# Strassen's seven products for both projections, dealt to the engines by a planner

## Chip, core and metric

The kernel runs on one core of one Trainium2 chip. The metric is the device time of one execution in microseconds (us), lower is better. Engines are named as the profile names them: PE multiplies matrices, DVE (VectorE), ACT (ScalarE) and POOL (GpSimd) do elementwise work, SP only issues transfers (DMA).

## What is computed

One layer of a decoder trunk in float32: `x` is 1024 x 2048, `w_in` 2048 x 6144, `w_out` 2048 x 2048.

```python
h = einsum('bsd,de->bse', x, w_in)                 # 1024 x 2048 x 6144
q, k, v, u_pool, gate = split(h, [1024, 2048, 3072, 4096])
attn = dilated_attention_mixture(rotary(q), rotary(k), v)   # 8 heads of 128
pool_out = grouped(causal_mean(u_pool, (2, 4, 8, 16)) - u_pool, w_pool) * pool_scale
y = concatenate([attn, pool_out]) * silu(gate)
out = einsum('bse,ed->bsd', y, w_out)              # 1024 x 2048 x 2048
x = layer_norm(2 ** 0.25 * x + out) * ln_gain + ln_bias
```

## The kernel before

**Products.** PE reads numbers in a shortened 32-bit type (fp32r), so each float32 tile is split in two: `hi`, a copy by ACT (L108, `ACT.activation(hi, src, AF.Copy)`), and `lo`, the rest, by DVE (L109, `DVE.tensor_tensor(out=lo, in0=src, in1=hi, op=ALU.subtract)`, two inputs in on-chip memory, SBUF). A product of two tiles is then three matmuls, `hi*hi + hi*lo + lo*hi`, added up in a bank of PSUM (512 columns each, 8 banks).

**Input projection.** `x` is loaded and split once at the start and stays in SBUF (`h`, `l`). The weights come in pieces of 128 x 512 (`Pieces`), loaded by SP (L127) and split up to four pieces ahead of their use. One block of 128 output columns after another runs over all 16 slices `kc` of 128 rows: q, k, u and gate blocks with the weights stationary and 512 columns of `x` moving (L640), value blocks with `x` stationary and 256 columns moving (L633). A block leaves PSUM once, when its 16 slices are done.

```python
for n, (a, b) in enumerate(((wh, xh), (wh, xl), (wl, xh))):
    for f in range(2):
        c = slice(f * 512, f * 512 + 512)
        PE.matmul(t[f], a[:, es], b[kc][:, c], start=kc == 0 and n == 0,
                  stop=kc == KC - 1 and n == 2)
```

**The second stream.** Attention of a head (L317 to L403: scores, softmax, transposes, products with the values) and pooling (L437 to L516) are cut into steps that `Background` lays between the units of the projection: `bg.tick()` after each slice. The order is thus fixed in the source. POOL does 32 multiplications for the rotary turn (L265, 32 x 512), a few fills, the roots of the norm (L681) and four pieces of the last norm (L710, L713).

**Output projection and norm.** `y` goes through DRAM (`y_d`), is split, and `mm3` (L731) multiplies it with pieces of `w_out`, four blocks of 128 tokens per piece. `residual` (L670, L671) adds `x` and takes the statistics; `norm` (L684, L688) centres and scales 512 columns at a time on DVE. The last 128 tokens are done in two halves of 256 columns, so that what is left behind the last matmul is one row block: `whole()` shares it between DVE, POOL and ACT.

Of the kernel before, what the change touches and what calls it, by code (L numbers as in the profile page):

```python
# [32 lines left out]
class Background:  # L33
    """Steps of a second stream, laid between the units of the first."""

    def __init__(self, rate):
        self.steps = deque()
        self.rate = rate
        self.credit = 0.0
        self.held = []  # L40

    def later(self, fn, ticks):
        self.held.append([ticks, fn])

    def flush(self):
        for _, fn in self.held:
            fn()
        self.held = []

    def add(self, fn, tag=None):  # L50
        self.steps.append((fn, tag))

    def tick(self):
        for h in self.held:
            h[0] -= 1
        while self.held and self.held[0][0] <= 0:
            self.held.pop(0)[1]()
        if not self.steps:
            self.credit = 0.0
            return  # L60
        self.credit += self.rate
        while self.credit >= 1.0 and self.steps:
            self.credit -= 1.0
            self.steps.popleft()[0]()

    def drain(self, tag=None):
        if tag is not None and all(t != tag for _, t in self.steps):
            return
        while self.steps:
            fn, t = self.steps.popleft()  # L70
            fn()
            if tag is not None and t == tag:
                return
# [3 lines left out]
def kernel(  # L77
    ctx: ExitStack,
    tc: tile.TileContext,
    x_t: bass.AP,  # L80
# [23 lines left out]
    v_d = [dram.tile([6 * P, 2 * P], F32, name=f"v_d{c}") for c in range(2)]
    gp_d = [dram.tile([P, S], F32, name=f"gp_d{c}") for c in range(4)]

    def split(hi, lo, src):
        ACT.activation(hi, src, AF.Copy)  # L108
        DVE.tensor_tensor(out=lo, in0=src, in1=hi, op=ALU.subtract)  # L109

    class Pieces:
        """Weights in pieces of 512 columns: loaded, then split, ahead of their use."""

        def __init__(self, sources, n_raw, n_split):
            self.sources = sources
            self.n_raw = n_raw
            self.n_split = n_split
            self.raw = deque()
            self.ready = deque()
            self.loaded = 0  # L120
            self.made = 0
            self.done = 0

        def load(self):
            if self.loaded < len(self.sources):
                t = wp.tile([P, 512], F32, name="w_raw", bufs=self.n_raw)
                SP.dma_start(t, self.sources[self.loaded])  # L127
                self.raw.append(t)
                self.loaded += 1

        def split(self):
            if self.made < len(self.sources):
                t = self.raw.popleft()
                hi = wp.tile([P, 512], F32R, name="w_hi", bufs=self.n_split)
                lo = wp.tile([P, 512], F32R, name="w_lo", bufs=self.n_split)
                split(hi, lo, t)
                self.ready.append((hi, lo))
                self.made += 1
                self.load()

        def load_first(self, between):
            t = wp.tile([P, 512], F32, name="w_raw", bufs=self.n_raw)
            SP.dma_start(t[:, 0:P], self.sources[0][:, 0:P])
            between()
            SP.dma_start(t[:, P:], self.sources[0][:, P:])
            self.raw.append(t)
            self.loaded = 1

        def split_first(self, between):
            t = self.raw.popleft()  # L150
            hi = wp.tile([P, 512], F32R, name="w_hi", bufs=self.n_split)
            lo = wp.tile([P, 512], F32R, name="w_lo", bufs=self.n_split)
            split(hi[:, 0:P], lo[:, 0:P], t[:, 0:P])
            between()
            split(hi[:, P:], lo[:, P:], t[:, P:])
            self.ready.append((hi, lo))
            self.made = 1
            self.load()

        def fill(self):  # L160
            while self.made < len(self.sources) and self.made - self.done < self.n_split:
                self.split()

        def take(self):
            while not self.ready:
                self.split()
            return self.ready.popleft()

        def retire(self):
            self.done += 1  # L170
# [701 lines left out]
```

## Time and profile before

| | us |
|---|---|
| three timed runs | 1565.46, 1565.57, 1566.03 |
| median of them | 1565.57 |
| span of the profiled execution, first to last instruction | 1564.2 |
| PE busy in it | 1551.0 (99%) |
| DVE, ACT, POOL busy | 631.6, 446.2, 54.6 |

The span is the whole of what the profile has of its execution; the median lies 1.4 us above it, for what is around the first and last instruction. Busy time of PE is the union of its matmuls, each of which is shown longer than the distance to the next one, because they are pipelined.

### The profile page before, as it was taken

The numbers are of one execution on the slowest core, as the hardware profiler recorded it, in microseconds if no ns is written. First come the engines' busy times: TensorE is split into PE (matmuls) and PEld (weight loads), VectorE is DVE, ScalarE is ACT, GpSimd is POOL, SyncE is SP. The second block draws the span as 40 slices with busy tenths as digits, with TensorE's granted clock in tenths as the row PEclk, the third lists the DMA queues.
The fourth block names the chain that finished last, engine by engine and source line by source line (L and its number), as shares of the span: only waits on it lengthen the run. The fifth ranks groups of instructions, "written<-read, shape, count | busy, mean of one in ns | idle before, by whom it ended". The sixth has DMA issues, their size and how long they took to land.

```text
span 1564.2 us, 20097 instructions
## 1 busy us (share of the span) xinstructions
PE 1551.0 (99%) x8116; PEld 1308.5 (84%) x8116; DVE 631.6 (40%) x1155; ACT 446.2 (29%) x788; POOL 54.6 (3%) x59
## 2 busy tenths in 40 slices
PE   9999999999999999999999999999999999999997
PEld 7898889888899888998888888888888888888886
DVE  4362433233441434424342113454153435476446
ACT  4333232142431323323323113222132424222310
POOL 0010100001000000000000000000000000000001
PEclk9999999999999999999999999999999999999999
DMA  7431213311124111241111222222213557357512
GB/s 239 146 110 34 61 41 89 107 35 41 54 68 128 41 41 54 60 117 57 38 54 54 68 75 84 97 75 61 61 54 114 167 205 242 115 197 242 146 52 104
DMA packets 73085, 149.75 MB, mean 96 GB/s; under 512 B 8288, under 2 KB 12256, under 8 KB 71712
## 3 DMA queue, kind: packets, MB, share of 16 engines
q1 hardware_dynamic: 72704, 148.19, 30.6%
q8 instruction: 63, 1.03, 0.3%
q10 hardware_dynamic: 288, 0.29, 0.1%
q14 instruction: 30, 0.25, 0.1%
HBM read 126.42 MB, written 22.02 MB: 95 GB/s over the span
## 4 chain that ended last, share of the span: by engine, by line
PE 98%; DVE 1%; ACT 1%; issue 0%; DMA 0%; DVEq 0%; SPq 0%
PE mm_ps L640 54%; PE mm_ps L731 10%; PE mm_ps L633 10%; PE s_ps L731 6%; PE o_ps L731 3%; PE t_ps L731 3%; PE s_ps L633 1%; PE s_ps L502 1%; PE s_ps L320 1%; PE o_ps L381 1%; PE o_ps L396 1%; PE s_ps L327 1%; PE o_ps L640 1%; PE o_ps L397 1%; PE t_ps L640 1%; PE t_ps L368 0%
## 5 line engine op out<-in xcount | busy, mean ns | idle before, releaser
L109 DVE TENSOR_TENSOR w_lo<-w_raw,w_hi 128x512 fp32r<-128x512 f32 (+1 forms) x337 | 234.3, 696 | 643.8 <-ACT w_hi L108 643.7
L108 ACT ACTIVATE w_hi<-w_raw 128x512 fp32r<-128x512 f32 (+1 forms) x337 | 212.0, 630 | 806.0 <-PE mm_ps L640 426.3
L640 PE MATMUL mm_ps<-h,w_hi 128*128 128x512 f32 x1248 | 395.9, 398 | 0.0
L640 PE MATMUL mm_ps<-l,w_hi 128*128 128x512 f32 x1248 | 386.1, 391 | 0.0
L640 PE MATMUL mm_ps<-h,w_lo 128*128 128x512 f32 x1248 | 386.0, 390 | 0.0
L640 PEld LDWEIGHTS mm_ps<-h,w_lo 128*128 128x128 f32 x1248 | 234.6, 188 | 50.3
L640 PEld LDWEIGHTS mm_ps<-l,w_hi 128*128 128x128 f32 x1248 | 234.5, 188 | 50.0
L640 PEld LDWEIGHTS mm_ps<-h,w_hi 128*128 128x128 f32 x1248 | 225.6, 188 | 45.7 <-issue 4.0
L633 PE MATMUL mm_ps<-w_hi,h 128*128 128x256 f32 x448 | 128.3, 286 | 0.0
L633 PE MATMUL mm_ps<-w_hi,l 128*128 128x256 f32 x448 | 126.8, 283 | 0.0
L633 PE MATMUL mm_ps<-w_lo,h 128*128 128x256 f32 x448 | 126.7, 283 | 0.0
L633 PEld LDWEIGHTS mm_ps<-w_hi,h 128*128 128x128 f32 x448 | 85.9, 192 | 0.5
L633 PEld LDWEIGHTS mm_ps<-w_lo,h 128*128 128x128 f32 x448 | 85.9, 192 | 0.1
L633 PEld LDWEIGHTS mm_ps<-w_hi,l 128*128 128x128 f32 x448 | 85.8, 192 | 0.0
L731 PE MATMUL mm_ps<-w_hi,h 128*128 128x512 f32 x192 | 74.7, 389 | 0.0
L731 PE MATMUL mm_ps<-w_lo,h 128*128 128x512 f32 x192 | 74.7, 389 | 0.0
L731 PE MATMUL mm_ps<-w_hi,l 128*128 128x512 f32 x192 | 74.7, 389 | 0.0
L731 PE MATMUL s_ps<-w_hi,h 128*128 128x512 f32 x128 | 49.8, 389 | 0.0
L731 PE MATMUL s_ps<-w_lo,h 128*128 128x512 f32 x128 | 49.8, 389 | 0.0
L731 PE MATMUL s_ps<-w_hi,l 128*128 128x512 f32 x128 | 49.8, 389 | 0.0
L342 ACT ACTIVATE p_t<-p_t,nm 128x128 f32<-128x128 f32 (+3 forms) x64 | 35.9, 562 | 32.1 <-DVE nm L335 31.7
L333 DVE CUSTOM_DVE_ANT_0 p_t<-s_ps,mask 128x128 f32<-128x128 f32 (+3 forms) x64 | 31.4, 490 | 28.1 <-PE s_ps L327 25.7
(176 smaller groups left out, 1704.7 us busy)
## 6 DMA issues: line engine op xcount, KB each, us to landing
w_raw<-in_w_in_dram SPq DMA_DIRECT2D x159, 256.0 KB, 2.7
w_raw<-in_w_out_dram SPq DMA_DIRECT2D x112, 256.0 KB, 2.7
w_raw<-in_w_v_dram SPq DMA_DIRECT2D x64, 256.0 KB, 2.7
z<-in_x_n_dram SPq DMA_DIRECT2D x8, 1024.0 KB, 5.1
p_t<-in_x_t_dram SPq DMA_DIRECT2D x15, 512.0 KB, 5.4
out_dram<-z SPq DMA_DIRECT2D x30, 256.0 KB, 3.4
y_d<-p_t SPq DMA_DIRECT2D x8, 512.0 KB, 3.8
y_d<-v_f SPq DMA_DIRECT2D x8, 512.0 KB, 3.5
```

The lines of the kernel that those rows point to most:

```text
L108: ACT.activation(hi, src, AF.Copy)
L109: DVE.tensor_tensor(out=lo, in0=src, in1=hi, op=ALU.subtract)
L320: PE.matmul(s[e][:, n - 2 * P:n], a[:, b * P:b * P + P], k[:, b * P - P:b * P + P], start=j == 0, stop=j == 2)
L327: PE.matmul(s[e][NF * r:NF * r + NF, :width(b) - 2 * P], qf[:, q0:q0 + NF], kv[:, :b - 1, r, :], start=True, stop=True, tile_position=(0, ...
L333: DVE.tensor_tensor_reduce(out=pt, in0=s[e][:, :n], in1=mask[:, NM - n:], op0=ALU.add, op1=ALU.max, scale=1.0, scalar=-3.0e38, accum_out=mx)
L342: ACT.activation(pt, pt, AF.Exp, scale=SCALE, bias=st.pop(("m", m, e)), accum_out=den)
L381: PE.matmul(o[:, 0:2 * P], v[:, 2 * m], p[:, 1:3], start=True, stop=False)
L396: PE.matmul(ov[:, e], v[:, 0, r], far_t[0][:, :, c], start=True, stop=False)
L397: PE.matmul(ov[:, e, 4:6], v[0:64, 1, r], far_t[1][:, :, c], start=False, stop=True)
L633: PE.matmul(o, x[kc][:, ss], y[:, es], start=kc == 0 and n == 0 and b % 2 == 0, stop=kc == KC - 1 and n == 2 and b % 2 == 1)
L640: PE.matmul(t[f], a[:, es], b[kc][:, c], start=kc == 0 and n == 0, stop=kc == KC - 1 and n == 2)
L731: PE.matmul(o, a[:, k % 2, ss], b, start=k == 0 and n == 0, stop=k == KC - 1 and n == 2)
```

## The change

**Seven products.** Each big product is cut in 2 x 2 quarters and done by Strassen's scheme (in the form with few sums): seven products of quarters and sums of quarters in place of eight. A *unit* is one of the seven for one piece of output: 4 slices x 3 matmuls of 512 columns in one bank (`mul_pair` for q, k, u, gates; `mul_wide` with `x`, and `y` in the output projection, stationary). There are 448 units: 20 pairs of blocks x 7 x 2 halves of the inner dimension, values 4 x 7 x 2, output 16 x 7. That is 5376 matmuls of 512 columns.

**What it adds.** Sums of quarters of `x`, `w_in`, `w_v`, `w_out` and `y` are made on the chip, nearly all on POOL (`combine`, L369; `w_out`'s and half of `x`'s are made early and laid in DRAM; `y`'s at L691). Every sum or quarter is split as before (L356, L359). Every unit's result leaves PSUM and is added into one or more quarters of the output: the first by an ACT copy (L404) and POOL sums, the others by DVE adds with one input in PSUM (L398). All 20 pairs are done for the first half of the inner dimension (phase A), laid in DRAM (`q_d`) and read again for the second half (phase B). The output projection comes in phases C and D, for attention and pooling. The scores are one float32 matmul instead of three fp32r ones (L762). The rotary turn moves from POOL to transfers and DVE (L717 to L723). The norm of the last four row blocks falls together at the end.

**The planner.** `Plan.op` records every operation with its engine, a due key and a cost in us; `place` gives the tiles their slots; `arrange` deals the operations to engines by a list schedule over those costs, and the program is written in that order. An engine runs its own list in order. Three banks serve a pair's seven units: product 2 is added onto product 1 in its bank, so it has to wait for the ACT copy of product 1; 7 and 4 go onto 6; 3 goes onto 5.

```diff
-class Background:
-    """Steps of a second stream, laid between the units of the first."""
...
+    LATE = {"PE": 1.2, "DVE": 0.3, "ACT": 0.3, "POOL": 0.3, "SP": 0.3}
+
+    def arrange(self):
...
+                    pick = r[0][2]
...
+                    o.start, o.end = t, t + cost
+                    free[e] = o.end
...
+        return sorted(out, key=lambda o: (o.start, o.seq))
...
+PAIRS = [("u", 0), ("g", 0), ("u", 1), ("p", 0), ("u", 2), ("u", 3), ("qk", 0), ("g", 1), ("qk", 1), ("qk", 2),
+         ("g", 2), ("qk", 3), ("qk", 4), ("g", 3), ("qk", 5), ("qk", 6), ("qk", 7), ("p", 1), ("p", 2), ("p", 3)]
...
+    def split(key, t, name, prio=None, lo=0, n=512, into=None):
...
+        def left():
+            DVE.tensor_tensor(out=c.lo(), in0=t.f(lo, lo + n), in1=c.hi(), op=ALU.subtract)
...
+    def combine(eng, key, a, b, alu, name, prio=None, into=None):
+        t = sb(name) if into is None else into
+
+        def go():
+            ENG[eng].tensor_tensor(out=t.f(), in0=a.f(), in1=b.f(), op=alu)
...
+        def take(self, i):
+            name = "abc"[{1: 0, 2: 0, 6: 1, 7: 1, 4: 1, 5: 2, 3: 2}[i]]
+            new = i in (1, 6, 5)
+            if new:
+                self.bank[name] = bank("mm")
+            return self.bank[name], new
...
+            if i == 1:
+                self.x = sb("x1")
+                self.copy(u, self.x, 0, 0, t)
+                if self.loaded:
+                    for q in (1, 3, 2):
+                        self.add("POOL", u, q, self.x)
+                return
+            if self.loaded:
+                self.add("DVE", u, {2: 0, 6: 1, 3: 1, 5: 3, 7: 3, 4: 2}[i], t)
...
+            s[1] = combine("POOL", k1, raw[2], raw[3], ADD, "w_sum")
+            s[2] = combine("POOL", k2, s[1], raw[0], SUB, "w_sum")
+            s[3] = combine("POOL", k3, raw[0], raw[2], SUB, "", into=raw[2])
...
+                    s[4] = combine("POOL", k4, raw[1], s[2], SUB, "", into=raw[1])
...
+                for n, (a, b) in enumerate(((w.hi(), x.hi()), (w.hi(), x.lo()), (w.lo(), x.hi()))):
+                    PE.matmul(o.f(), a[:, es], b, start=new and kc == 0 and n == 0, stop=kc == 3 and n == 2,
+                              skip_group_check=True)
...
+            seq += [(n, 1)] + ([(n - 1, 4)] if n > n0 else []) + [(n, i) for i in (6, 5, 2, 7, 3)]
...
+            if last and d != 3 or not last and d % 2:
...
+                op("DVE", u + 1.4 + 0.3 * d, V5, centred, [mv, gain[d // 2]], [t])
+                op("DVE", u + 1.6 + 0.3 * d, V5, scaled, [rs, bias[d // 2]], [t])
+            else:
...
+                op("ACT", u + 1.8, A5, normal, [nb, rs], [t])
+                op("POOL", u + 2, G5, gained, [gain[d // 2]], [t])
+                op("POOL", u + 2.2, G5, biased, [bias[d // 2]], [t])
```

Three places in the lists of engines. First POOL at the start of the program, before the change (`far_t` is a fill, the rest the rotary turn of head 0):

```order
L240 MEMSET far_t_98 128x768
L241 MEMSET far_t_99 64x256
L265 ISA
L265 TENSOR_TENSOR k_f<-k_f,rope 32x512 x2
L265 TENSOR_TENSOR q_f<-q_f,rope 32x512 x4
```

The same place on POOL in the changed kernel (`x_sum` and `w_sum` are sums of quarters; sums that write `w_raw` overwrite a quarter that is no longer needed):

```order
L369 TENSOR_TENSOR x_sum<-x_raw 128x512 x3
L369 TENSOR_TENSOR w_sum<-w_raw 128x512
L369 TENSOR_TENSOR w_sum<-w_sum,w_raw 128x512
L369 TENSOR_TENSOR x_sum<-x_raw 128x512
L369 TENSOR_TENSOR w_sum<-w_raw 128x512
L369 TENSOR_TENSOR w_sum<-w_sum,w_raw 128x512
L369 TENSOR_TENSOR w_sum<-w_raw 128x512
L369 TENSOR_TENSOR w_sum<-w_sum,w_raw 128x512
L369 TENSOR_TENSOR w_raw<-w_raw 128x512 x3
L369 TENSOR_TENSOR w_raw<-w_raw,w_sum 128x512 x3
```

POOL, which had two fills before its first real work, now has sums to make that the fifth and later products of the first pairs are split from.

Second, DVE in phase A of the changed kernel, about one pair's worth (`q` is a quarter of output, `x_1547` the copy of product 1, `mm` a bank):

```order
L398 TENSOR_TENSOR q<-x_1547,mm 128x512
L359 TENSOR_TENSOR w<-w_raw,w 128x512
L398 TENSOR_TENSOR q<-x_1547,mm 128x512
L359 TENSOR_TENSOR w<-w_sum,w 128x512 x2
L359 TENSOR_TENSOR w<-w_raw,w 128x512
L398 TENSOR_TENSOR q<-q,mm 128x512
L359 TENSOR_TENSOR w<-w_raw,w 128x512 x2
L398 TENSOR_TENSOR q<-q,mm 128x512
L359 TENSOR_TENSOR w<-w_raw,w 128x512
L398 TENSOR_TENSOR q<-x_1547,mm 128x512
```

Before, DVE's list in the projection is splits (`w_lo`, `w_raw` and `w_hi` in SBUF) and a head's steps between them:

```order
L399 TENSOR_TENSOR p_t<-o_ps,p_t 128x2x6x32
L403 TENSOR_TENSOR p_t<-p_t,gate 128x1024
L109 TENSOR_TENSOR w_lo<-w_raw,w_hi 128x512 x12
L260 STREAM_SHUFFLE k_f<-mm_ps 32x512 x2
L264 TENSOR_TENSOR mm_ps<-mm_ps,rope 32x512 x2
L109 TENSOR_TENSOR w_lo<-w_raw,w_hi 128x512
L269 TENSOR_TENSOR mm_ps<-mm_ps,k_f 32x512 x2
L274 TENSOR_TENSOR k_lo<-mm_ps,k_hi 128x512
```

An add that frees a bank, which came once for 16 slices, now stands between any two splits.

Third, DVE behind the last matmul. Before, from the add of the last half row block on:

```order
L670 SCALAR_TENSOR_TENSOR z<-z,s_ps 128x256
L671 BN_STATS stats<-z 128x6
L679 BN_AGGR mv<-stats 128x2
L680 TENSOR_SCALAR rs<-mv 128x1
L704 TENSOR_SCALAR neg<-mv 128x1
L684 SCALAR_TENSOR_TENSOR z<-z,mv,gain 128x512 x2
L688 SCALAR_TENSOR_TENSOR z<-z,rs,bias 128x512
L684 SCALAR_TENSOR_TENSOR z<-z,mv,gain 128x464
L688 SCALAR_TENSOR_TENSOR z<-z,rs,bias 128x512
L688 SCALAR_TENSOR_TENSOR z<-z,rs,bias 128x464
```

And in the changed kernel, from the add of the last unit on, up to the statistics of the last row block (after these rows, 10 more of L1069 and L1073 follow):

```order
L398 TENSOR_TENSOR z<-z,mm 128x512
L1069 SCALAR_TENSOR_TENSOR z<-z,mv,gain 128x512
L1061 SCALAR_TENSOR_TENSOR nb<-mv,rs 128x1
L1069 SCALAR_TENSOR_TENSOR z<-z,mv,gain 128x512
L1073 SCALAR_TENSOR_TENSOR z<-z,rs,bias 128x512 x2
L1069 SCALAR_TENSOR_TENSOR z<-z,mv,gain 128x512
L1073 SCALAR_TENSOR_TENSOR z<-z,rs,bias 128x512
L1069 SCALAR_TENSOR_TENSOR z<-z,mv,gain 128x512 x2
L1073 SCALAR_TENSOR_TENSOR z<-z,rs,bias 128x512 x2
L1043 BN_STATS stats<-z 128x6
L1054 BN_AGGR mv<-stats 128x2
L1055 TENSOR_SCALAR rs<-mv 128x1
```

The norm of two row blocks stands ahead of the statistics of the last two, so four row blocks are finished where one was; POOL's list has 12 sums of 128x512 for the same four.

## Rows read from the trace of the kernel before

**Rows 1.** The page: span, busy time of each engine; the chain that ended last.

```profile
span 1564.2 us, 20097 instructions
...
PE 1551.0 (99%) x8116; PEld 1308.5 (84%) x8116; DVE 631.6 (40%) x1155; ACT 446.2 (29%) x788; POOL 54.6 (3%) x59
...
PE 98%; DVE 1%; ACT 1%; issue 0%; DMA 0%; DVEq 0%; SPq 0%
```

**Rows 2.** The chain in order of time: start, length (us), matmuls with 512 and 256 columns.

```profile
by line: PE mm_ps L640 54.1%; PE mm_ps L731 10.4%; PE mm_ps L633 10.4%; PE s_ps L731 6.3%; PE t_ps L731 2.8%; PE o_ps L731 2.8%; PE s_ps L633 1.5%; PE s_ps L502 1.4%; PE s_ps L320 1.3%; PE o_ps L381 0.9%; PE o_ps L396 0.9%; PE s_ps L327 0.8
...
74.77 23.04 PE mm_ps L633 x192
...
1248.02 43.52 PE mm_ps L731 x192
```

**Rows 3.** Timeline of PE's first products: start, length, engine, line.

```profile
4.60 0.76 PE L640 MATMUL t_ps<-h,w_hi 128*128 128x512 f32 x1
...
6.78 0.63 PE L640 MATMUL o_ps<-l,w_hi 128*128 128x512 f32 x1
7.21 0.63 PE L640 MATMUL t_ps<-h,w_lo 128*128 128x512 f32 x1
```

**Rows 4.** Groups by line and shape: count, busy us, mean ns, idle time before.

```profile
L109 DVE TENSOR_TENSOR w_lo<-w_raw,w_hi 128x512 fp32r<-128x512 f32 x335 | 233.5, 698 | 640.7 <-ACT w_hi L108 640.7
...
L108 ACT ACTIVATE w_hi<-w_raw 128x512 fp32r<-128x512 f32 x335 | 211.1, 631 | 805.3 <-PE mm_ps L640 426.3 <-PE o_ps L731 86.7 <-PE mm_ps L633 83.5
...
L265 POOL TENSOR_TENSOR k_f<-k_f,rope 32x512 f32<-32x512 f32 x16 | 20.2, 1281 | 386.9 <-DVE k_f L260 386.9
...
L274 DVE TENSOR_TENSOR k_lo<-mm_ps,k_hi 128x512 fp32r<-128x512 f32 x16 | 10.7, 686 | 9.2 <-ACT k_f L271 9.2
```

**Rows 5.** Timeline of DVE, 90.6 to 94.5 us.

```profile
91.32 1.24 DVE L109 TENSOR_TENSOR w_lo<-w_raw,w_hi 128x512 fp32r<-128x512 f32 x1
92.48 0.68 DVE L264 TENSOR_TENSOR t_ps<-t_ps,rope 32x512 f32<-32x512 f32 x1
```

**Rows 6.** Timeline of POOL in the same stretch.

```profile
90.72 2.98 POOL L265 TENSOR_TENSOR q_f<-q_f,rope 32x512 f32<-32x512 f32 x2 [8.23 <-DVE q_f L260]
```

**Rows 7.** Timeline of DVE in the end, 1540 to 1565 us.

```profile
1543.63 0.74 DVE L684 SCALAR_TENSOR_TENSOR z<-z,mv,gain 128x512 f32<-128x512 f32 x1
...
1553.32 0.42 DVE L670 SCALAR_TENSOR_TENSOR z<-z,s_ps 128x256 f32<-128x256 f32 x1 [2.62 <-PE s_ps L731]
...
1556.02 1.28 DVE L688 SCALAR_TENSOR_TENSOR z<-z,rs,bias 128x512 f32<-128x512 f32 x1
1557.22 1.19 DVE L684 SCALAR_TENSOR_TENSOR z<-z,mv,gain 128x464 f32<-128x464 f32 x1
1558.33 2.38 DVE L688 SCALAR_TENSOR_TENSOR z<-z,rs,bias 128x512 f32<-128x512 f32 x2
```

**Rows 8.** Timeline of POOL in the end; PE's last matmul.

```profile
1555.82 2.10 POOL L710 TENSOR_TENSOR z<-z,gain 128x288 f32<-128x288 f32 x2
1557.88 2.35 POOL L713 TENSOR_TENSOR z<-z,bias 128x288 f32<-128x288 f32 x2
...
1553.01 0.28 PE L731 MATMUL s_ps<-h,l 128*128 128x256 f32 x1
```

**Rows 9.** Transfers: the queue's share (page), a load's time to land, SP's issue (ns).

```profile
q1 hardware_dynamic: 72704, 148.19, 30.6%
...
w_raw<-in_w_in_dram SPq DMA_DIRECT2D x159, 256.0 KB, 2.7
...
L127 SPq DMA_DIRECT2D w_raw<-in_w_in_dram x159: 327/328/548, 2.6 to 1161.7; - x159
```

**Rows 10.** Windows: busy us (count) of each engine, PE's clock, transfers' share, GB/s.

```profile
0.00:10.00 10.00, 7.93 (x15) 4.78 (x16) 3.53 (x6) 4.78 (x8) 1.18 (x6) 1.00 0.76 250
...
1400.00:1420.00 20.00, 20.00 (x90) 16.57 (x89) 16.50 (x28) 3.69 (x6) 1.43 (x2) 1.00 0.88 291
1540.00:1564.00 24.00, 13.29 (x104) 12.78 (x102) 15.50 (x25) 2.00 (x4) 6.29 (x6) 0.84 0.26 97
```

More of the change, by code (lines that the diff above doesn't have):

```diff
@@ L27, with __init__, f @@
 EPS = 1e-5
-Q0, K0, U0, G0 = 0, 8, 16, 24
 NF = 32
 NM = 6 * NF + 2 * P
-class Background:
[L36 to L73, printed above, removed]
+class Buf:
+    def __init__(self, plan, space, size, parts=1, name="t", dtype=F32):
+        self.plan, self.space, self.size, self.parts, self.name, self.dtype = plan, space, size, parts, name, dtype
+        self.seq = plan.count()
+        self.slot = self.tile = None
+        self.writer = [None] * parts
+        self.readers = [[] for _ in range(parts)]
+        self.ops = []
+        self.heads = []
+    def f(self, lo=0, hi=None):
+        if self.tile is None:
+            kind, n = self.slot
+            pool, size, _ = self.plan.kinds[kind]
+            self.tile = pool.tile([P, self.size], self.dtype, name=self.name, tag=f"{kind}_{n}", bufs=1,
+                                  padded_shape=[P, size])
+        return self.tile[:, lo:self.size if hi is None else hi]
@@ L76 @@
+N1, N2 = 10, 50
 @with_exitstack
@@ L104 @@
[L104 to L170, printed above, removed]
@@ new lines, in mul_wide, with go @@
+    def mul_wide(units, i, u, fixed, moving):
+        banks = [x.take(i) for x in units]
+        k = len(units)
+        for kc in range(4):
+            m = moving[kc]
+            for n, (o, new) in enumerate(banks):
+                s, c0 = fixed(n, kc)
+                def go(kc=kc, m=m, s=s, c0=c0, o=o, new=new):
+                    c1 = c0 + P
+                    for j, (a, b) in enumerate(((s.hi(c0, c1), m.hi()), (s.hi(c0, c1), m.lo()), (s.lo(c0, c1), m.hi()))):
+                        PE.matmul(o.f(), a, b, start=new and kc == 0 and j == 0, stop=kc == 3 and j == 2,
+                                  skip_group_check=True)
+                op("PE", u + 0.25 * (kc * k + n), MM3, go, m.both + s.both, [o])
+        for n, x in enumerate(units):
+            x.after(i, u + k - 0.25 * (k - 1 - n))
@@ L314, in scores, with score @@
+        ks = [k0 + 3.6 + 2.6 * m for m in range(4)]
+        for m in range(4):
+            k = ks[m]
+            ws_ = [width(2 * m), width(2 * m + 1)]
+            po = (0, ws_[0])
+            pt = sb("p_t", sum(ws_), 2)
+            mx, nm, den, rd = sm("mx", 2, 2), sm("nm"), sm("den", 2, 2), sm("rd")
+            banks = [bank("s_ps") for _ in range(2)]
+            def score(e, s, m=m):
                 b = 2 * m + e
```

1380 lines of the change are left out of this document (826 added, 554 removed).

## The prediction

> **What bounds the kernel now.** I read the page first: PE is busy 1551.0 of 1564.2 us, and the chain that ended last is PE for 98% [rows 1]. So the time is PE's work plus a start and an end of some 13 us; DVE, ACT and POOL have room (40%, 29%, 3%). Then the chain in order of time, for what a matmul really costs: 192 matmuls of 512 columns take 43.52 us, 0.2267 us each, and 192 of 256 columns 23.04 us, 0.120 each [rows 2]. Only the first few, still at the lower of the clock's two levels, are 0.43 us apart [rows 3]. Last the groups by shape, for the prices of the operations that the change multiplies [rows 4], and the two places where DVE and POOL work at the same time [rows 5 to 8].
>
> **PE: what goes and what stays.** Before, the projections are 40 blocks x 16 x 6 = 3840 matmuls (L640), 1440 and 96 halves (L731; 1536 in all, of which 48 were cut in two), 96 for pooling, all at 0.2267 (halves 0.120), and 1536 of 256 columns (L633) at 0.120. That is 870.5 + 337.3 + 11.5 + 21.8 + 184.3 = 1425.4 us, where the full-width ones of L731 are 1488. The remaining 125.6 of 1551.0 us are attention, the warm-up and the slow first matmuls. After: 448 units x 12 = 5376, and 96 for pooling, 5472 x 0.2267 = 1240.5 us. The remainder stays, less some 8 us: the warm-up goes, the slow first matmuls are taken below. The scores cost more: L320's three fp32r products are 1.3% of the span, 20.3 us for 56; one float32 product of that size costs L381's 0.9% / 32 = 0.44 us, 56 of them 24.6, so +4. PE needs 1240.5 + 121.5 = **1362 us**, 189 less than now.
>
> **The others.** What covers the new work is PE's time, so I count each list with the row of its kind. DVE: about 756 operations with both inputs in SBUF (636 splits, the norm, window sums) at 0.69 for 512 columns, 538 us; 352 adds out of PSUM at 0.686 [rows 4], 242; attention and statistics some 127: 907 us, two thirds of PE's. ACT: some 630 us by 0.631 per split. POOL: 476 sums; a row of 512 columns takes it 1.28 us [rows 4], 623 us with the longer ones. The row is of 32 partitions. With 128, two of the norm's multiplications of 288 columns take 2.10 us [rows 8], of which some 0.25 is waiting for the DVE step between them; (2.10 - 0.25) / 2 x 512 / 288 = 1.65. I take 1.28, the row with the same number of columns, and keep up to 1.65 for the range. SP issues 1134 transfers at 0.33 us, 370 us. They carry 283 MB instead of 148; the latter took 30.6% of the transfer engines over the span [rows 9], so by bytes 65% of a span of 1400 us. None of these sums is a bound over the whole; the question is where they meet.
>
> **Where DVE and POOL meet.** At 91.32 us a split takes 1.24 us instead of 0.69, under a POOL multiplication that began at 90.72; the next POOL one ends at 93.70 instead of 93.25 [rows 5, 6]. A DVE operation in between, with one input in PSUM, takes 0.68 as always [rows 5]. In the end it goes to and fro: DVE's centring and scaling steps, 0.74 alone, take 1.2 to 1.3 and start 1.1 to 1.2 apart, one POOL operation between two of them [rows 7, 8]. So a DVE operation with two SBUF inputs and a POOL sum exclude each other. From 91.32: DVE's last 0.69 us begin at 91.87, 1.15 after POOL's start; POOL ends 1.14 after DVE. A pair takes about 1.7 us, of which I give DVE 0.6 and POOL 1.1. [...]
>
> Both together over the whole: 756 x 0.6 + 476 x 1.1 = 977 us of some 1400. I laid the lists side by side in the program's order and counted what DVE and POOL have been given between two of PE's 6064 matmuls:
> - *Start.* By the 200th matmul (45 us of PE): 56 two-input operations and 23 sums, 58.9 us, from 4.6 us on, when the first product starts [rows 3]. That is 13.6 more than PE has. Some of it is for units that come later; but products also run at half clock at first, 0.2 us more each for some 20. The 31 loads that stand there, 8.1 MB, take 32 us at the 250 GB/s of the first 10 us [rows 10] and hide. I take **12**, between 3 and 23 (both whole durations, 68.1 us).
> - *Middle.* In the densest 40 us of phases A and B (from the 2471st matmul), 30 and 21: 41 us against 40. Else it is 16 to 39. Weights are due 3.5 units, 9.5 us, ahead. **4**, between 0 and 20.
> - *B to C.* Just before and after the output projection starts (4714th to 4888th matmul, 40 us): 34 and 26, 49 us. **6**, between 0 and 11.
> - *End.* Behind the 5905th matmul PE has 160 left, 36 us; DVE has 58 two-input operations and POOL 33 sums, 34.8 + 36.3 = 71 us. DVE alone has 60. After the last result leaves DVE the stores take 3.5 us (1560.7 to 1564.2 before, when 1558.33 + 2.38 is taken for the first [rows 7]). So 71 + 3.5 - 36 = 38.5 from the last matmul to the end; before it was 11.2 (from 1553.01 [rows 8]). By DVE alone 27, and less if all hides: DVE's 20 steps at 0.74, with statistics, root and stores, 23. I take **38**, between 23 and 51 (POOL at 1.65).
>
> **Sum.** 1362 + 4.6 to the first product + 12 + 4 + 6 + 38 = 1426.6 of span, against 1564.2, and 1.4 around it: **1428 us**.
>
> **Rivals.**
> 1. *The helpers hide.* The planner runs them so far ahead that exclusion costs nothing before the end: 1362 + 4.6 + 3 + 23 + 1.4 = 1394. For it: 977 of 1400 us, and only 41 in the densest stretch of the middle. Against: the start has nothing to run ahead of, and the end's order is fixed.
> 2. *POOL is slower on 128 partitions*, 1.65 a sum and 1.5 of the shared time. Then 40 us stretches of the middle want up to 50, 64 us too much in all from the 440 us mark to 1040 and beyond, the start 19, the end 51: 1362 + 4.6 + 19 + 64 + 51 + 1.4 = 1502. For it: the 288 columns in rows 8. Against: those were themselves waiting for DVE.
> 3. *The transfers bind at B to C.* From 1000 to 1160 us of PE time the lists issue 53 MB; at 291 GB/s, the best 20 us now [rows 10], that is 183 us, 23 too many: 1451. Against: that stretch was not full, 0.88.
> 4. *It gets slower: the banks.* Product 2 waits for its bank until ACT has copied product 1 out, 7 until 6 is added, 3 until 5. Two units lie between, 5.4 us; the result is seen at once (0.03 us after the last matmul at 1553.29 [rows 7, 8]) and the add takes 0.69, so 4.7 us of delay is free. If adds stand behind splits that wait for POOL longer than that, PE stops in each unit. To lose the whole gain, 1568 - 1428 = 140 us over 448 units, each must wait 0.31 us, so adds must be 5.0 us late on average. DVE would have to be backlogged by seven operations throughout; at two thirds of its time I do not see it.
>
> Before, 16 slices went by between two evacuations of a block, so no row shows such a wait; the order alone says it can come.
>
> **How the numbers follow.** 0.50 for the forecast (1405 to 1450 by its own terms), 0.20 for rival 1 (1385 to 1405), 0.19 for rival 2 (1450 to 1510), 0.07 for rival 3 (1440 to 1465), 0.04 for rival 4. To hold 8 in 10 the range leaves out the far half of rival 2, rival 4 and the low edge of rival 1: 1388 to 1480. A measurement of this kernel can tell about 0.2% (3 us) from no change, the three runs lying within 0.6 us. Faster by more 0.95, within 0.01, slower 0.04.
>
> **What would show it.** In the profile after: PE's rows at 0.2267 apart and a PE need near 1362 us where nothing waits; L479 and L496 with 5376 matmuls as the chain's bulk. Step by step: DVE's splits (L359) at 0.69 in the quiet stretches and up to 1.3 or more where POOL works; POOL's L369 near 1.3 (rival 2: 1.6 and more); in the first 65 us PE idle 10 to 15 us, waiting for DVE or ACT splits; in the middle PE's share 9 in all slices (rivals 2 and 4: 7 or 8, waits of L479 for L398); SP or DMA as releaser of splits around B to C (rival 3); and between the last matmul and the end 30 us or more in which DVE and POOL alternate. I would be wrong if PE idles in the middle by more than 20 us, or its clock falls there to the lower level, as it is granted only 0.84 in the last stretch now [rows 10], because waits break up its work; then a stretch costs up to twice its matmuls, which no row prices.

## The result, and the profile after

The changed kernel takes 1520.95 us (median of four runs, 1518.54 to 1522.38), the kernel before 1565.74 beside it: a ratio of 0.9712, 95% interval 0.9698 to 0.9725. It is faster, but only by 45 us of the 138 that were forecast, and it lies 41 us above the range. The page of the changed kernel, which answers to [rows 1, 9]; of part 2 the shares in 40 slices of 38 us, and PE's granted clock in the same slices:

```profile
span 1518.5 us, 19395 instructions
...
PE 1419.3 (93%) x6472; PEld 1126.0 (74%) x6472; DVE 1083.6 (71%) x1536; ACT 586.5 (39%) x1052; POOL 739.5 (49%) x499
...
PE   7899999999999999999999999999995999999780
...
DVE  7964546445456777989866759587885766878988
...
q1 hardware_dynamic: 171200, 283.52, 58.0%
...
PE 24%; DVE 6%; POOL 1%; DMA 1%; issue 1%; ACT 0%; SPq 0%; DVEq 0%; POOLq 0%
```

PE was 99% busy and 98% of the chain; now it is 93% busy, with holes in the first two slices, in the thirty-first and in the last three. (The chain can be followed back only to 1006 us this time, so its 24% for PE is not to be set beside the 98%.) DVE and POOL have worked 177 and 116 us longer than the 907 and 623 of the forecast. The groups, which answer to [rows 4], show where:

```profile
L359 DVE TENSOR_TENSOR w<-w_raw,w 128x512 fp32r<-128x512 f32 x368 | 345.8, 963 | 77.3 <-ACT w L356 74.8 <-PE mm L479 0.3
L359 DVE TENSOR_TENSOR w<-w_sum,w 128x512 fp32r<-128x512 f32 x112 | 119.9, 1078 | 30.6 <-ACT w L356 29.6
L369 POOL TENSOR_TENSOR w_raw<-w_raw 128x512 f32<-128x512 f32 x40 | 65.3, 1635 | 0.5
L398 DVE TENSOR_TENSOR q<-q,mm 128x512 f32<-128x512 f32 x72 | 48.7, 685 | 41.9 <-PE mm L479 32.1 <-PE mm L496 9.4
L780 DVE TENSOR_SCALAR nm<-mx 128x2 f32<-128x2 f32 x32 | 15.1, 471 | 1.1
```

The splits (L359, two inputs in SBUF) take 0.96 to 1.08 us in the mean instead of 0.69, POOL's sums 1.41 to 1.74 by group, while DVE's additions out of PSUM (L398) stay at 0.685. Whom PE waits for is in the view of PE's waits (us in total, times, longest):

```profile
PE mm L496 <- DVE w L359: 18.7, 7, 9.5
PE mm L496 <- ACT w L356: 11.9, 1, 11.9
PE mm L479 <- ACT w L356: 8.3, 1, 8.3
PE s_ps L760 <- DVE qk L723: 7.8, 3, 5.3
...
PE mm L496 <- DVE z L398: 2.5, 2, 1.4
```

The 8.3 is the way to the first matmul: SP issues four loads of `x` from 0.74 us on and the first weight at 2.59, and ACT splits that at 7.63. The windows of 40 us that have the holes (columns as in [rows 10]):

```profile
0.00:40.00 40.00, 29.76 (x113) 23.02 (x114) 32.41 (x29) 21.85 (x36) 24.49 (x19) 0.96 0.57 205
...
1120.00:1160.00 40.00, 27.11 (x116) 20.86 (x115) 26.28 (x29) 13.75 (x23) 33.83 (x23) 0.85 0.95 350
...
1400.00:1440.00 40.00, 30.45 (x128) 24.25 (x126) 37.34 (x56) 18.04 (x29) 18.69 (x14) 0.89 0.65 212
1440.00:1480.00 40.00, 31.80 (x113) 23.12 (x112) 35.44 (x39) 8.60 (x14) 20.81 (x13) 0.81 0.42 137
1480.00:1518.00 38.00, 3.54 (x16) 2.55 (x14) 32.32 (x40) 4.56 (x6) 21.75 (x16) 0.58 0.30 111
```

The clock column is part of the loss: the trace records PE's granted clock at two levels, 1.00 and 0.50, and after a hole PE's matmuls run at 0.50 for a while. In the median the projection matmuls start 0.427 us apart while it is 0.50 and 0.231 while it is 1.00. And two places of the timeline, B to C and the end:

```profile
1149.79 1.59 POOL L691 TENSOR_TENSOR y_sum<-y,y_sum 128x512 f32<-128x512 f32 x1
...
1151.41 0.32 SPq L318 DMA_DIRECT2D ys_d<-y_sum  x1
1151.77 0.46 SPq L318 DMA_DIRECT2D w_raw<-in_w_out_dram  x1
...
1157.26 1.27 ACT L356 ACTIVATE w<-w_raw 128x512 fp32r<-128x512 f32 x2 [0.37 <-DMA w_raw<-in_w_out_dram]
...
1157.94 0.80 PE L496 MATMUL mm<-w,c 128*128 128x512 f32 x1 [11.93 <-ACT w L356]
...
1433.53 1.71 POOL L1082 TENSOR_TENSOR z<-z,gain 128x512 f32<-128x512 f32 x1
...
1434.04 1.21 DVE L1061 SCALAR_TENSOR_TENSOR nb<-mv,rs 128x1 f32<-128x1 f32 x1
...
1435.83 1.75 DVE L359 TENSOR_TENSOR w<-w_raw,w 128x512 fp32r<-128x512 f32 x1
...
1437.64 2.93 PE L496 MATMUL mm<-w,c 128*128 128x512 f32 x6 [9.55 <-DVE w L359]
```

At B to C a POOL sum ends at 1151.38, SP issues its store at 1151.41 and only then, 0.36 us later, the load of a weight that ACT splits at 1157.26 and for which PE has waited 11.93 us. In the end DVE does nine centring and scaling steps of rows 0 to 3 from 1423.29 on, some of them at 1.6 to 1.8 us because POOL works at the norm too, and only then, at 1435.83, the split for which PE has waited 9.55 us.

Last, the chain in order of time, one long stretch without any wait and two pieces of the tail:

```profile
1174.03 215.58 PE mm L496 x933
...
1487.44 1.75 DVE z L1069
1489.19 3.33 DVE z L1073 x2
```

That is 231.1 ns for a matmul, where the forecast had 226.7, and 1.67 to 1.75 us for a DVE step with a POOL step between, as forecast.

**The miss, divided.** I took PE's matmuls from start to start: a distance above 0.6 us is a wait, what a matmul has above its usual distance while the granted clock is 0.50 is clock, the rest is PE's own pace. (The trace has no record of the clock before 11.5 us; the first seven matmuls, 0.43 us apart as they are later where 0.50 is recorded, are counted as at that level.) In the span of 1518.5 us: 8.3 to the first matmul, 1395.8 at its own pace, 61.1 of waits, 17.9 of clock, 35.3 from the start of the last matmul to the end. By place, beside the terms of the sum:

| term | forecast | measured | of it waits, clock |
|---|---|---|---|
| PE's own work | 1362 | 1395.8 | |
| to the first product | 4.6 | 8.3 | |
| start, 0 to 100 us | 12 | 14.3 | 8.6, 5.7 |
| middle, 500 to 1100 us | 4 | 19.2 | 14.8, 4.4 |
| B to C, 1100 to 1200 us | 6 | 19.5 | 16.9, 2.6 |
| end | 38 | 60.0 | 19.6, 5.1, and 35.3 |
| elsewhere | 0 | 1.3 | 1.3, 0 |

The difference is 92 us: 34 of pace, 22 in the end, 15 in the middle, 14 from B to C, 6 in the start with the way to the first product, 1 elsewhere.

### The profile page after: what moved, and what is told of

It reads as the page before. It is cut to its first block, busy times and chain, and to the rows that moved or that the text cites. A ratio compares the mean times of both kernels' runs of the same rounds, so it can differ in the third digit from the quotient of the medians.

```text
span 1518.5 us, 19395 instructions
## 1 busy us (share of the span) xinstructions
PE 1419.3 (93%) x6472; PEld 1126.0 (74%) x6472; DVE 1083.6 (71%) x1536; ACT 586.5 (39%) x1052; POOL 739.5 (49%) x499
## 5 line engine op out<-in xcount | busy, mean ns | idle before, releaser
L479 PE MATMUL mm<-c,w 128*128 128x512 f32 x3360 | 825.4, 401 | 21.8 <-ACT w L356 8.3
L479 PEld LDWEIGHTS mm<-c,w 128*128 128x128 f32 x3360 | 626.8, 190 | 171.9 <-issue 8.6
L496 PE MATMUL mm<-w,c 128*128 128x512 f32 x2016 | 478.0, 399 | 34.7 <-DVE w L359 18.7
L496 PEld LDWEIGHTS mm<-w,c 128*128 128x128 f32 x2016 | 383.1, 191 | 129.3 <-DVE w L359 23.3
L359 DVE TENSOR_TENSOR w<-w_raw,w 128x512 fp32r<-128x512 f32 x368 | 345.8, 963 | 77.3 <-ACT w L356 74.8
L356 ACT ACTIVATE w<-w_raw 128x512 fp32r<-128x512 f32 x368 | 226.6, 628 | 359.4 <-DMA w_raw<-in_w_in_dram 90.4
L359 DVE TENSOR_TENSOR w<-w_sum,w 128x512 fp32r<-128x512 f32 x112 | 119.9, 1078 | 30.6 <-ACT w L356 29.6
L369 POOL TENSOR_TENSOR w_sum<-w_raw 128x512 f32<-128x512 f32 x56 | 83.2, 1487 | 109.7 <-DMA w_raw<-in_w_in_dram 27.2
L369 POOL TENSOR_TENSOR f_sum<-f_raw 128x512 f32<-128x512 f32 x40 | 58.9, 1476 | 129.3 <-DVE w L359 44.2
L356 ACT ACTIVATE w<-w_sum 128x512 fp32r<-128x512 f32 x112 | 69.7, 629 | 134.2 <-POOL w_sum L369 109.9
L398 DVE TENSOR_TENSOR q<-x,mm 128x512 f32<-128x512 f32 x72 | 49.1, 685 | 86.5 <-PE mm L479 61.1
L398 POOL TENSOR_TENSOR z<-z,x 128x512 f32<-128x512 f32 x24 | 38.1, 1622 | 121.0 <-ACT x L404 121.0
L369 POOL TENSOR_TENSOR w_raw<-w_raw,w_sum 128x512 f32<-128x512 f32 x40 | 62.4, 1561 | 63.5 <-DVE w L359 34.9
L369 POOL TENSOR_TENSOR f_sum<-f_raw,f_sum 128x512 f32<-128x512 f32 x40 | 60.5, 1513 | 66.9 <-issue 24.4
L369 POOL TENSOR_TENSOR w_sum<-w_sum,w_raw 128x512 f32<-128x512 f32 x48 | 68.9, 1435 | 25.9 <-PE t_ps L803 11.0
L398 DVE TENSOR_TENSOR q<-q,mm 128x512 f32<-128x512 f32 x72 | 48.7, 685 | 41.9 <-PE mm L479 32.1
L404 ACT ACTIVATE x<-mm 128x512 f32<-128x512 f32 x64 | 38.0, 596 | 90.2 <-PE mm L479 36.4
L359 DVE TENSOR_TENSOR c<-y_raw,c 128x256 fp32r<-128x256 f32 (+1 forms) x84 | 57.0, 716 | 12.4 <-ACT c L356 12.2
L369 POOL TENSOR_TENSOR w_raw<-w_raw 128x512 f32<-128x512 f32 x40 | 65.3, 1635 | 0.5
L398 DVE TENSOR_TENSOR qk<-qk,mm 128x512 f32<-128x512 f32 x48 | 32.7, 682 | 34.8 <-PE mm L479 34.8
L398 DVE TENSOR_TENSOR z<-z,mm 128x512 f32<-128x512 f32 x64 | 42.3, 682 | 19.3 <-PE mm L496 19.2
L359 DVE TENSOR_TENSOR c<-x_raw,c 128x512 fp32r<-128x512 f32 x40 | 37.3, 943 | 24.6 <-ACT c L356 24.6
```

The source lines that it names most:

```text
L356: ACT.activation(c.hi(), t.f(lo, lo + n), AF.Copy)
L359: DVE.tensor_tensor(out=c.lo(), in0=t.f(lo, lo + n), in1=c.hi(), op=ALU.subtract)
L369: ENG[eng].tensor_tensor(out=t.f(), in0=a.f(), in1=b.f(), op=alu)
L398: ENG[eng].tensor_tensor(out=o, in0=o if base is None else base.f(), in1=src.f(), op=ADD)
L404: ACT.activation(dst.f(lo, lo + 512), src.f(), AF.Copy)
L479: PE.matmul(o.f(), a[:, es], b, start=new and kc == 0 and n == 0, stop=kc == 3 and n == 2, skip_group_check=True)
```

## Experiments

Twelve runs, each against the kernel before on the same chip. Times are medians; the ratio of the changed kernel is 0.9712, and 0.0064 of ratio are 10 us.

**Where tiles lie.** The program gives its tiles addresses. In the kernel before, all activations and weights of the projections start at the same place modulo 512 bytes. In the changed kernel a 256-byte and a 96-byte tile lie between its large slots, so that these fall in two groups, 352 bytes (the other way 160) apart. I sorted 4978 projection matmuls (those 220 to 260 ns before the next one) by the groups of the tile that they read and of the next stationary tile, which is loaded meanwhile (0.19 us in the mean for L479 and L496): 2662 with both in one group are 229.6 ns apart, 2316 across groups 233.5. It is the next stationary tile that counts and not the one in use: where the two lie in different groups, 111 matmuls that agree with their own tile alone are 234.7 ns from the next, 104 that agree with the next one alone 230.7.

```diff
-    plan.slots("sm", "g", sb_pool, 64, 2)
+    plan.slots("sm", "g", sb_pool, 104, 2)
```

> One number is changed: a reserved slot of 64 words is made 104, so that the 352 bytes that lay between the two groups of large slots become 512, and every large tile starts at the same place modulo 512 bytes. The order of all instructions stays. Theory (where the moving tile and the next stationary tile start): in the changed kernel, of 4978 neighbouring projection matmuls between 220 and 260 ns apart, the 2316 whose two tiles lie in different groups are 233.5 ns apart and the 2662 in the same group 229.6. With one group all of them should be between 227.7 (the kernel before, where all are in one group) and 229.6: 5376 times 1.8 to 3.7 ns, 10 to 20 us off, 1501 to 1511 us. Rival (the pace comes from something else, such as the semaphores or the shorter runs into one bank): the spacing stays at 231.4 and the time within 3 us of 1521.

1503.63 us, 0.9603 (0.9588 to 0.9617): 17 us off, by one number and with every instruction in its place. A long stretch of the chain, as above:

```profile
1169.82 202.88 PE mm L496 x895
```

226.7 ns now; over all projection matmuls 227.3, nine tenths of them at 228 or less, against 28% in the changed kernel. PE's own pace is 1373.6 us instead of 1395.8. The waits grew from 61.1 to 65.8, since a faster PE meets the same lists. The reverse, on the kernel before, with one unused tile ahead of the weights:

```diff
-    wp = ctx.enter_context(tc.tile_pool(name="wp", bufs=1))
+    wp = ctx.enter_context(tc.tile_pool(name="wp", bufs=1)); wp.tile([P, 88], F32, name="shift")
```

> The kernel before with one unused tile of 352 bytes ahead of the weights, so that the weights start 352 bytes off the activations modulo 512, where they agreed; nothing else is changed. Theory (addresses): the 3744 matmuls of L640 go from 227.7 to about 233.5 ns and those of L731 from 226.7 to about 233, 22 + 10 us more, 1590 to 1605 us; the 256-column ones of L633 may add up to 10. Rival (the slower pace of the changed kernel has to do with its shorter units): 1566 us as before.

1597.25 us, 1.0202 (1.0185 to 1.0219), 31 us slower. First a row of L640 in the chain of the kernel before, then the chain of this run, for that and for the 43.52 us of 192 in [rows 2]:

```profile
985.73 39.47 PE mm_ps L640 x174
```

```profile
1001.84 40.76 PE mm_ps L640 x174
...
1271.34 44.80 PE mm_ps L731 x192
```

233.3 ns each for L731 instead of 226.7, and 234.3 for L640 instead of 226.8. So the address is the cause, and the shorter units are not. Two more runs ask whether a smaller distance between the groups makes the difference too; the slot is 136 and 120 words.

> The changed kernel with a reserved slot of 136 words instead of 64, so that the two groups of large tiles lie 128 bytes apart modulo 512 instead of 160 (or 352, the other way round); order and all else as in the changed kernel, nothing is left out. It asks what size the address rule has. If tiles only have to agree modulo 128 bytes (or less), all projection matmuls are about 227 ns apart as in the run with one group, 1500 to 1507 us. If they have to agree modulo 256 or 512, the 2405 pairs across the groups stay at 233 to 234 ns and the time at 1518 to 1524 us.

> The same with a slot of 120 words, the groups 64 bytes apart. If tiles only have to agree modulo 64 bytes, 227 ns everywhere and about 1503 us; otherwise the pairs across the groups stay at 233 to 234 ns and the time near 1521 us.

1516.63 us (0.9684, 0.9670 to 0.9699) and, in a single run, 1514.52: neither answer. At 128 bytes pairs across the groups are 232.1 ns apart in the mean; at 64 bytes 230.5 with the stationary tile in the lower group and 233.1 the other way. Agreement modulo 64 or 128 bytes is thus not enough in these runs; no run has the groups 256 bytes apart, and why the distance matters was not shown.

**DVE and POOL.** POOL keeps its place, its order and its time, but reads nothing:

```diff
-            ENG[eng].tensor_tensor(out=t.f(), in0=a.f(), in1=b.f(), op=alu)
+            [POOL.memset(t.f(), 0.0) for _ in range(3)] if eng == "POOL" else ENG[eng].tensor_tensor(out=t.f(), in0=a.f(), in1=b.f(), op=alu)
...
-                POOL.tensor_tensor(out=t.f(), in0=x.f(xlo, xlo + 512), in1=z.f(zlo, zlo + 512), op=alu)
+                [POOL.memset(t.f(), 0.0) for _ in range(3)]
```

and the same for POOL's additions in L398.

> Left out: POOL's sums and its additions of the first product. In their place POOL writes zeros into the same tile three times (estimated 1.5 us by the 0.739 us of a 128x768 memset, so POOL is not relieved), so that it reads nothing from SBUF; the gates and the norm stay. The output is therefore not the reference's. Theory (DVE and POOL exclude each other and that makes splits late): the splits of L359 fall from a mean of 0.96 to 1.08 us to about 0.70, DVE from 1083.6 to about 950 us busy, and PE's waits at the start, in the middle and from B to C from some 43 us (with 13 more of lower clock) to under 15: 1470 to 1490 us. Rival (those waits come from transfers that SP issues in order, or from banks that are not yet evacuated): splits get shorter but the waits stay, 1510 to 1521 us.

1479.88 us, 0.9454 (0.9438 to 0.9469), 41 us off, POOL as busy as ever. The first fence is the page's busy times, the second the groups, the third the longest of PE's waits from B to C:

```profile
PE 1403.5 (95%) x6472; PEld 1120.9 (76%) x6472; DVE 888.0 (60%) x1536; ACT 583.9 (40%) x1052; POOL 744.0 (50%) x1315
```

```profile
L359 DVE TENSOR_TENSOR w<-w_raw,w 128x512 fp32r<-128x512 f32 x368 | 255.9, 718 | 94.1 <-ACT w L356 93.4
L359 DVE TENSOR_TENSOR w<-w_sum,w 128x512 fp32r<-128x512 f32 x112 | 80.2, 726 | 38.0 <-ACT w L356 37.6
...
L780 DVE TENSOR_SCALAR nm<-mx 128x2 f32<-128x2 f32 x32 | 12.0, 375 | 1.1
```

```profile
PE mm L496 <- ACT w L356: 12.5, 1, 12.5
```

Splits are at 0.72 us, DVE at 888 us, near the 907 of the forecast. Waits and clock at the start fall from 14.3 to 2.3 us, in the middle from 19.2 to none above 0.6 us. From B to C they stay, 16.7 and 3.5. Ahead of the last matmul, where POOL still does the norm, they are 17.7 instead of 24.7. So exclusion is the cause at the start and in the middle, and not from B to C, where the expectation was wrong. Beside a POOL that only writes, then, splits are hardly held up: 0.718 and 0.726 us in the mean, where they take 0.963 and 1.078 in the changed kernel.

The next run gives the sums to DVE, really done:

```diff
-            s[1] = combine("POOL", k1, raw[2], raw[3], ADD, "w_sum")
+            s[1] = combine("DVE", k1, raw[2], raw[3], ADD, "w_sum")
```

and so for all calls of `combine` and for the sums of y.

> All 312 sums of weights, x and y that POOL made are made by DVE, at the planner's price for DVE; nothing is left out. DVE's own work grows by 312 x 0.69 = 215 us, POOL's falls by some 400. Theory (a POOL sum that meets a DVE operation costs DVE up to 1.1 us of waiting, more than the 0.69 that DVE needs to do it): DVE's waiting of 177 us falls by about two thirds, DVE is busy about 1185 us of the span, and PE waits less where DVE and POOL were both dense: 1490 to 1510 us. Rival (the sums stand ahead of the splits in DVE's queue and DVE, at four fifths of the span, becomes late itself): 1530 us and more.

The page's busy times, and PE's waits for rotated keys:

```profile
PE 1415.3 (94%) x6472; PEld 1126.5 (75%) x6472; DVE 1142.2 (76%) x1848; ACT 584.1 (39%) x1050; POOL 273.3 (18%) x187
```

```profile
PE s_ps L760 <- DVE qk L723: 10.8, 3, 7.5
```

1503.51 us, 0.9604 (0.9589 to 0.9618), 17 us off. DVE does 312 operations more, 215 us of work, and is busy only 59 us longer (1142.2 against 1083.6); POOL's 466 us had spared it no more than that. The waits fall to 3.1 us at the start and 9.1 from B to C; in the middle they stay (14.0, and 7.6 of clock). Of these, 10.8 are for rotated keys (second fence; 7.8 in the changed kernel). Which step on the way to them holds them, the transfers of the turn or DVE's steps L719 and L723, was not taken apart.

**B to C.** The sums that only phase D reads, later:

```diff
-        o = c - 4
+        o, k = c - 4, k + (16 if c >= 8 else 0)
```

> The sums of y for the second half (c from 8 on), which only phase D reads, and their loads and stores get a key 16 units later; nothing is left out. Theory (from B to C POOL makes these sums back to back, SP's queue stands behind their stores, and the loads of the output weights behind them arrive too late, 12.3 us of waiting at 1146 us): most of the 16.9 us of waits and 2.6 us of lower clock between 1100 and 1200 us go, 1503 to 1510 us. Rival (the transfers themselves are the limit there, 0.95 of the DMA engines at 350 GB/s between 1120 and 1160 us): the waits stay or move by a few us, 1516 to 1524 us.

1507.83 us, 0.9633 (0.9619 to 0.9647), 13 us off. The window of the hole:

```profile
1120.00:1160.00 40.00, 34.51 (x146) 27.07 (x145) 25.59 (x32) 15.51 (x27) 23.61 (x15) 0.96 0.93 332
```

and the longest wait that is left:

```profile
PE mm L496 <- ACT c L356: 5.5, 1, 5.5
```

PE is busy 34.5 us in it instead of 27.1, with the transfers nearly as full. Waits from B to C are 7.2 us instead of 16.9, the clock 2.7. So more than half of what stood there was SP's list behind POOL's sums, not the transfers; the rest, mostly one wait for a split of `y`, was not followed further.

Prices alone do not do it:

```diff
-V5, A5, G5, MM3 = 0.76, 0.64, 1.45, 0.682
+V5, A5, G5, MM3 = 0.76, 0.64, 1.6, 0.682
...
-        op("DVE", key, 0.16 + 0.6 * n / 512, left, [t, c.both[0]], c.both[1:], prio=prio)
+        op("DVE", key, 0.16 + 0.85 * n / 512, left, [t, c.both[0]], c.both[1:], prio=prio)
```

> The changed kernel with two of the planner's prices raised to what the trace shows where DVE and POOL meet: a split on DVE 1.01 instead of 0.76, a POOL sum 1.6 instead of 1.45. Nothing is left out; only the order that the planner gives the engines and SP's queue changes. Theory (the lateness is partly one of order: the planner does not know that the two engines exclude each other, so loads stand behind stores that come late): the 16.9 us of waits from B to C shrink, 1505 to 1515 us. Rival (the lateness is one of demand, DVE and POOL simply have too much to do together in those stretches): 1518 to 1525 us.

1518.95 us, 0.9700 (0.9685 to 0.9715): the same as the changed kernel within the intervals. The waits from B to C are 14.9 us. That is the time of the rival (demand), but the run before shows some 10 us of it to be order after all. The keys decide which sum comes first there, and a dearer sum does not change its key.

**The end.** Gain and bias of two column blocks go to PSUM, and DVE's two steps read them there:

```diff
+                for n in range(4):
+                    t = in_ps[n % 2, 1 + n // 2 * 2] = bank("g_ps")
+                    op("ACT", first + 42 + -2, A5, lambda t=t, n=n: ACT.activation(t.f(), gains[n % 2][n // 2].f(512, 1024), AF.Copy),
+                       [gains[n % 2][n // 2]], [t])
...
+                gd = in_ps[0, d] if d % 2 else gain[0]
...
-                    DVE.scalar_tensor_tensor(out=zf(st, d), in0=zf(st, d), scalar=mv.f(0, 1), in1=gain[d // 2].f(512 * (d % 2), 512 * (d % 2) + 512),
+                    DVE.scalar_tensor_tensor(out=zf(st, d), in0=zf(st, d), scalar=mv.f(0, 1), in1=gd.f(0, 512),
```

(the bias alike; in the last two rows the block that POOL takes is the third instead of the fourth).

> Alone on the changed kernel; nothing is left out. ACT copies columns 512 to 1023 and 1536 to 2047 of gain and bias into four PSUM banks before the last group, and DVE's centring and scaling of these columns reads them there, so that it has one input in SBUF and one in PSUM, as L398 has, which POOL never held up (0.682 to 0.685 us). Theory (in the end DVE and POOL exclude each other): 16 DVE steps of rows 0 to 3 at 0.75 instead of 1.25 us get the last splits through 8 to 11 us sooner, and behind the last matmul 20 DVE steps and 12 POOL steps run side by side, 15 to 19 us instead of 27.5: 35.3 us from the last matmul becomes about 27, the 25 us of waits and lower clock between 1400 and 1483 some 15 to 20; 1502 to 1511 us. Rival (the four banks taken from the units make PE wait, or the end is set by something else, such as the order of rows): 1517 us or more.

1505.07 us, 0.9617 (0.9603 to 0.9632), 16 us off. DVE and POOL in its timeline, where the changed kernel has 1.7 us for each step:

```profile
1488.84 0.74 DVE L1071 SCALAR_TENSOR_TENSOR z<-z,mv,g_ps 128x512 f32<-128x512 f32 x1
1489.62 0.75 DVE L1075 SCALAR_TENSOR_TENSOR z<-z,rs,g_ps 128x512 f32<-128x512 f32 x1
...
1489.13 1.27 POOL L1084 TENSOR_TENSOR z<-z,gain 128x512 f32<-128x512 f32 x1
1490.48 1.27 POOL L1087 TENSOR_TENSOR z<-z,bias 128x512 f32<-128x512 f32 x1
```

Both at their own pace, side by side. From the last matmul to the end it is 26.1 us instead of 35.3, as expected; waits and clock ahead of it 16.1 and 4.0 instead of 19.6 and 5.1.

**Together.** Three of the edits (addresses, sums on DVE, late sums of y), then gain and bias in PSUM too, then the norm of rows 0 to 3 behind the splits:

> The edits of the three runs before together: large tiles all at one place modulo 512 bytes, all sums on DVE, the sums of y for c from 8 on 16 units later. Nothing is left out. If the causes are separate, their gains add: 1521 - 17.3 - 17.4 - 13.1 = 1473 us. Since two of them cure the same wait from B to C (16.9 us became 9.1 and 7.2), 1474 to 1486 is what the theories together give. Rival (PE runs faster and DVE, busy about 1140 us, becomes late everywhere): 1490 us or more, with PE's waits above 60 us.

> As the run before it in this list, and gain and bias in PSUM too. Nothing is left out. By the theory of the end 10 to 19 us less than that run: 1457 to 1474 us. Rival: no gain, because DVE has the sums and is itself the bound at the end.

```diff
-                op("DVE", u + 1.4 + 0.3 * d, V5, centred, [mv, gd], [t])
+                op("DVE", u + 1.4 + 0.3 * d, V5, centred, [mv, gd], [t], prio=None if st > 3 else u + 9)
```

> As the run before it in this list, and the last steps of the norm of rows 0 to 3 get a priority 9 units later, so that the splits of the last group go first on DVE. Nothing is left out. Theory (PE waits in the last group because these steps stand ahead of the splits on DVE): the remaining waits between 1380 and 1450 us fall below 5 us, the steps move into gaps and partly behind the last matmul; 0 to 8 us less than the run before it. Rival (DVE has no gaps there): the tail behind the last matmul grows by as much as the waits fall, the same time within 3 us.

They take 1476.28 (0.9427, 0.9413 to 0.9441), 1461.38 (0.9327, 0.9311 to 0.9342) and 1459.85 us (0.9328, 0.9314 to 0.9342). Three edits give 45 us, where the single gains add to 48; with the fourth it is 60. The third step gives nothing, and the view of waits says why; first the run ahead of it has

```profile
PE mm L496 <- DVE w L359: 9.8, 5, 5.7
...
PE mm L496 <- DVE z L398: 3.0, 2, 1.5
```

and the last one in their place

```profile
PE mm L496 <- DVE z L398: 11.9, 5, 3.8
...
PE mm L496 <- DVE w L359: 2.8, 2, 2.6
```

DVE has no gap there, and what is put behind the splits makes the banks late instead. From the last matmul to the end it is 24.5 us against 26.1, so the tail did not grow, as the rival had it. The fastest kernel is thus 7% below the kernel before and 4% below the changed one.

## Why the prediction was wrong, step by step

- **PE, 1362 us: too small by 34.** The count of matmuls was right; the step that failed is "5472 x 0.2267". The row of 192 matmuls of L731 was taken for a property of the shape, and it is one of shape and place. Of the 34 us, 22 go with the addresses (1395.8 to 1373.6). Most of the other 12 can be counted by line in the same traces, from start to start: attention's matmuls take 113.8 us against 102.3 before, where the forecast allowed 4 for the scores. L762 takes 29.3 us, 0.52 for each of 56 products where L381's 0.44 was taken, against L320's 22.8; the narrow products L767 take 15.4 against L327's 12.6. That is some 8 of the 12; the rest stays open.
- **Start, 12: right in kind and nearly in size**, 14.3 within 3 to 23, 2.3 without POOL's reading. Some of that is luck in the parts: 13.6 us of work too many were counted, and PE waited 8.6. The first product came 3.7 us later than before, since four loads of `x` stand ahead of its weight, which the sum left out.
- **Middle, 4: mis-sized, 19.2**, just within its bounds. The 41 of 40 us counted amounts of work in a stretch. PE waits for a particular split or rotated key, and such a one stands behind others (5.3 us at the longest for a key). Without POOL's reading nothing of it is left. The count also left out a one-input step that POOL holds up: L780, 0.17 us alone, takes 0.47 in the mean.
- **B to C, 6: wrong in kind, 19.5, outside its bounds.** The demand on DVE and POOL was counted, and SP's queue was not followed: stores of sums that nobody needs yet stood ahead of loads that PE needed. Moving the sums takes 10 of the 19.5 us away; taking the exclusion away takes none. With the sums on DVE as well (the run with three edits) 2.8 us of waits are left.
- **End, 38: the tail was near, 35.3, and what lies ahead of it was missing, 24.7.** The 36 us of PE's last 160 matmuls were taken as covered work. The steps of the norm of rows 0 to 3, alternating with POOL, stood ahead of the splits that these matmuls read. What was left out is in DVE's list: in the trace the 58 two-input operations take 66.9 us, and 41 others (adds out of PSUM, statistics, small steps) 21.6, which the sum of 71 did not have. With them it is 92.6, and 92.3 us go by from the 160th matmul from the end to DVE's last operation. That the tail alone came out near 38 is luck, for the sum had PE through its last 160 matmuls in 36 us, and it took 61.9.
- **The pair at 1.7 us** held: in the tail the chain's steps start 1.63 to 1.75 us apart where a POOL step stands between. The two whole durations one after the other, 0.74 [rows 7] and 1.28 [rows 4], would be 2.02; the rows do not bear that out.
- **Rivals.** Helpers that hide (1394): no. POOL slower on 128 partitions (1502): its time is nearest and its reason is wrong; alone it takes 1.27 to 1.30 us (1489.13 above), and is slow where DVE meets it. Transfers at B to C (1451): no, the run with three edits moves as much between 1100 and 1200 us (315 GB/s; the changed kernel 309) and waits 2.8 us there. Banks (1568): hardly, all waits for L398 are 8.7 us.
- **The sign for being wrong** was half given: waits and clock in the middle are 19.2 us and not above 20, but the granted clock does fall to 0.50 there, at 602 us for 3.4 and at 762 for 6.8. Its price over the whole is 17.9 us, and only the start's term had some of it.

So of the 92 us, 22 went to a duration that was taken for constant, 22 to DVE's operations in the end that the count left out, and 29 in the middle and from B to C to waits for single urgent operations that stand behind others, in DVE's list where POOL holds it up and in SP's; amounts of work in a stretch do not tell of those.

## What to carry to other kernels

When a kernel's matmuls are to be multiplied by a duration, look where the program puts the tiles of that row and of the new kernel; a small tile between large ones cost 22 us of PE's pace here, 17 of the time, and one number mends it. Giving a second engine work that excludes the first saved little here: POOL's 466 us of sums spared DVE 59, and moving one operand of 32 DVE steps to PSUM gave 16 us, nearly as much as moving 312 sums to DVE, 17. A sum of work in a window needs every operation of the list in it, and even then it is no price for a wait; for that, follow the queue of the transfer or operation that PE needs next, stores of others included.
